# Routing at the seam between attention and experts: order of the last tiles, and constant products on TensorE

## The chip, the cores and the metric

The kernel runs on one core of a Trainium2 chip. The metric is device time in microseconds of one execution; the figure given is the median of several runs. Besides the timed runs there is one profiled execution, from which all rows here are taken.

## The reference

One layer of an encoder over 1024 tokens of width 1024, all in float32. Two attention mixers and an output projection come first; then a mixture of experts, whose routing is the subject here.

```python
h = h + jnp.concatenate([oa, ob], axis=-1) @ w_out[l]
h = h + _hierarchical_moe(_rms_norm(h, norm2_g[l]), ...)
return _rms_norm(h, final_norm_g)

def _hierarchical_moe(x, ...):            # n = 1024 tokens, 4 groups of 8 experts, TOP_K = 2
    g_logits = xt @ router_group_w + router_group_b
    g_prob = jax.nn.softmax(g_logits); g_top_p, g_top = lax.top_k(g_prob, 1)
    e_logits = xt @ router_expert_w + router_expert_b      # those of the chosen group are kept
    e_top_logit, e_top = lax.top_k(e_in_group, TOP_K)
    gates = g_top_p * jax.nn.softmax(e_top_logit, axis=-1)
    # every token goes to its two experts: (silu(x @ w_gate[e]) * (x @ w_up[e])) @ w_down[e],
    # times its gate, added up per token
```

## The kernel before

Tokens stand in eight tiles of 128 (`NT` = 8). After the attention mixers the kernel runs a routing stage, one loop over the tiles, and then 32 experts, one after the other, each with up to 128 of its tokens in one block (blocks beyond that are made in a loop at the end).

**Routing.** For tile j, `projected(j, b)` (L965) makes half b of the output projection, twelve fp32r matmuls of 512 columns from `half_product` (L833), and adds the residual. With the second half it computes the norm's factor (`rstd` on POOL), normalises the tile into `xn` on VectorE (L982), and has SP store it to `xn_d` in HBM (L983). `routed(j)` (L987) is a generator whose `yield`s let the loop put its TensorE work in between. Its steps are: transposes of the tile's two halves (L994, two steps, evicted to `xt` by ScalarE); the router's logits as sixteen passes (L1000), then on VectorE the choice of group and of two experts (L1004 to L1031), which ends in the one-hot `ohb`; the counts `pc` of earlier tokens per expert (L1034, L1035), with the gates, and per choice a matrix `put` (token to place in its expert's list) and `what` (32 columns for the token's number, 32 for its gate); last the table's product `first_at` += `put` x `what` (L1064), two fp32 matmuls. The counts need the running sum `cum` of the tiles before. `turned` (L818) normalises and transposes tile j+1 of the second mixer.

TensorE's order is written out by hand (`manual_schedule`, L1078 to L1106); the other engines' order is made by a planner that simulates the program, and in which what stands earlier in the program goes first where both are ready. `issue_after(x)` makes what is in the block, on x's engine, come behind x. After the loop over j the order is: tile 7's second transposes and logits, tile 6's counts and table, tile 7's counts and table:

```python
            for j, n in ((NT - 1, 2), (NT - 2, 2), (NT - 1, 2)):
                for _ in range(n):
                    next(routes[j])
```

**The seam.** VectorE turns the table into row numbers and gates (L1118, L1119). POOL gathers the rows of expert 0 from `xn_d` by these numbers (L1173) into `x_g`, the storage of `o_b[0]`; then it issues three weight loads (L915) and `listed` (L1068): for each tile two indirect writes of token and gate into lists in HBM, `slot_d`, whose four tensors are used in turn, so that tile 2's writes wait for those of tile 0.

**Experts.** For expert e, TensorE transposes the gathered rows (`rows_in`, L1190); ScalarE and VectorE split rows and weights into a high and a low part (`split`, L141). Twelve units of weights (512 KB each) are used, with six matmuls of 512 columns for each: eight for gate and up (L1206), four for down (L1230), the latter put among the units of the next expert. In the gate-and-up product of expert e, after its sixth unit, the rows of expert e+1 are gathered and transposed (`KR` = 5). There is one `x_g`, so a gather waits for the transposes of the one before. Weights come by SP into 39 buffers in turn; six of them (`raw_b`) and the two splitting buffers lie where the routing stage's tiles lay, and wait until those have been read for the last time.

Of the kernel before, what the change touches and what calls it, by code (L numbers as in the profile page):

```python
# [39 lines left out]
MID = 2  # L40
# [75 lines left out]
def _all(t, n, offset=0):  # L116

    return _dram(t, offset, [[0, P], [1, n]])
# [8 lines left out]
def tile_encoder(ctx, tc, I, out):  # L127
# [3 lines left out]
    def act(o, i, f=AF.Copy, **kw):  # L131
        A.activation(o, i, f, **kw)  # L132
# [162 lines left out]
    def run(g):  # L295
        for _ in g:
            pass
# [491 lines left out]
    wr = outb.tile([P, 8, 36], F32, name="wr")  # L789
    nc.sync.dma_start(wr[:, :, 0:4], I["router_group_w"][0].rearrange("(k p) n -> p k n", p=P))  # L790
    nc.sync.dma_start(wr[:, :, 4:36], I["router_expert_w"][0].rearrange("(k p) n -> p k n", p=P))
# [3 lines left out]
    G.tensor_tensor(wr, wr, gk[:, :, None].to_broadcast([P, 8, 36]), op=OP.mult)  # L795
    br = outb.tile([P, 36], F32, name="br")
    nc.sync.dma_start(br[:, 0:4], _all(I["router_group_b"], 4))
    nc.sync.dma_start(br[:, 4:36], _all(I["router_expert_b"], 32))
# [153 lines left out]
    with tc.tile_pool(name="rt", bufs=1, side="right") as rt, \  # L952
# [7 lines left out]

        def mixed(j):

            tiles[j] = turned(o_b[j // 2][:, j % 2], 1, "a")

        def projected(j, b):  # L965
# [12 lines left out]
            V.tensor_tensor(ss[:, 6:7], ss[:, 4:5], ss[:, 5:6], op=OP.add)  # L978
            rstd(ss[:, 7:8], ss[:, 6:7], D)
            for b in range(2):  # L980
                bs = slice(512 * b, 512 * b + 512)
                V.scalar_tensor_tensor(xn[:, bs], h[b], ss[:, 7:8], g2[:, bs], op0=OP.mult, op1=OP.mult)  # L982
            stores.append(nc.sync.dma_start(xn_d[P * j:P * j + P], xn).ins)  # L983
            for b in range(2):
                nc.sync.dma_start(y_d[P * j:P * j + P, 512 * b:512 * b + 512], h[b])

        def routed(j):  # L987
# [10 lines left out]
            ps = bank("c", [P, 36])  # L998
# [11 lines left out]
            e4 = wo2.tile([P, 8], F32, name="e4")  # L1010

            V.tensor_scalar(r[:, 0:1], top[:, 0:1], -1.0, None, op0=OP.mult)
            act(e4[:, 0:4], lg[:, 0:4], AF.Exp, bias=r[:, 0:1], accum_out=r[:, 1:2])
# [22 lines left out]
            V.tensor_tensor(cum, cum, ob, op=OP.add)  # L1036
            V.reciprocal(r[:, 2:3], r[:, 1:2])
            V.tensor_tensor(r[:, 7:8], top2[:, 1:2], top2[:, 0:1], op=OP.subtract)
            act(r[:, 6:7], r[:, 7:8], AF.Exp)
            V.tensor_scalar(r[:, 7:8], r[:, 6:7], 1.0, None, op0=OP.add)  # L1040
            V.reciprocal(r[:, 7:8], r[:, 7:8])
            V.tensor_tensor(r[:, 8:9], r[:, 7:8], r[:, 2:3], op=OP.mult)
            V.tensor_tensor(r[:, 9:10], r[:, 8:9], r[:, 6:7], op=OP.mult)
            V.tensor_scalar(r[:, 10:11], small[:, 35:36], -1.0, float(S - P * j), op0=OP.mult, op1=OP.add)
            puts = []
            for k in range(2):
# [4 lines left out]
                put = wo2.tile([P, P], F32, name="put")  # L1051
                (V if j >= JV else G).tensor_scalar(put, slots, r[:, 12 + k:13 + k], None, op0=OP.is_equal)
                what = wo2.tile([P, 2, NE], F32, name="what")
                for n, col in enumerate((10, 8 + k)):
                    (V if j >= JV else G).tensor_scalar(what[:, n], oh[:, k], r[:, col:col + 1], None, op0=OP.mult)
                puts.append((put, what))
# [5 lines left out]
            yield  # L1062
            for k, (put, what) in enumerate(puts):
                T.matmul(first_at, put, what.rearrange("p a b -> p (a b)"), start=(j == 0 and k == 0),  # L1064
                         stop=(j == NT - 1 and k == 1), skip_group_check=True)
# [12 lines left out]
        with tc.manual_schedule(engines={mybir.EngineType.PE}):  # L1078
            tiles[0] = first_mixed
            for j in range(NT):  # L1080
                routes.append(routed(j))
                projected(j, 0)
                if j:
                    next(routes[j - 1])
                    next(routes[j - 1])
                if (MID == 0 or j == 0) and j + 1 < NT:
                    mixed(j + 1)
                if MID != 2 and j > 1:
                    next(routes[j - 2])
                projected(j, 1)  # L1090
                if MID == 2 and j > 1:
                    next(routes[j - 2])
                if j + 1 < NT:
                    if MID and j:
                        mixed(j + 1)
                else:
                    next(routes[j])
                if j:
                    next(routes[j - 1])
                if j > 1:  # L1100
                    next(routes[j - 2])
                if j and j % 2 == 0:
                    load_until(RC + 3 * j // 2 - 1)
            for j, n in ((NT - 1, 2), (NT - 2, 2), (NT - 1, 2)):
# [11 lines left out]
        rows = lst.tile([P, NE], I32, name="rows")  # L1116
        gate = lst.tile([P, NE], F32, name="gate")
        V.tensor_scalar(rows, first_at[:, 0:NE], -1.0, float(S), op0=OP.mult, op1=OP.add)  # L1118
        V.tensor_copy(gate, first_at[:, NE:2 * NE])  # L1119
# [50 lines left out]

    def load_rows(rows):

        gathers.append(G.indirect_dma_start(out=x_g, out_offset=None, in_=xn_d[:, :],  # L1173
                                            in_offset=bass.IndirectOffsetOnAxis(ap=rows, axis=0),
                                            bounds_check=S - 1, oob_is_err=False).ins)
        return x_g
# [83 lines left out]
    with tc.manual_schedule(engines={mybir.EngineType.PE}):  # L1260
        py, gathers = [], []
        before, xg = iter(()), load_rows(rows[:, 0:1])
# [4 lines left out]
        st = rows_in(xg)  # L1267
# [109 lines left out]
```

## Time and profile before

| what | us |
|---|---|
| median of three runs | 1386.3 (1386.0 to 1390.7) |
| profiled execution | 1382.0 |
| its span, first to last instruction | 1380.4 |
| TensorE busy in the span | 1287.7 (93%) |
| VectorE busy | 1160.4 (84%) |
| ScalarE busy | 941.9 (68%) |
| GpSimd (POOL) busy | 570.5 (41%) |

The page's slices show TensorE at nine tenths in nearly every slice, and the DMA engines near full from the routing stage to the end of the experts. In the rows below, a time is that from the start of the span; x16 behind a row means that many instructions merged, whose duration runs from the first's start to the last's end; the brackets hold the idle time of the engine before it and what ended it. TensorE's matmuls overlap, so the distance of two starts, not the duration, is what one costs.

### The profile page before, as it was taken

What the parts mean: (1) busy time and instruction counts of PE and PEld (TensorE: products, weight loads), DVE (VectorE), ACT (ScalarE), POOL (GpSimd) and SP (SyncE); (2) the same over time, 40 slices, a digit from 0 to 9 for tenths busy, and PEclk for the clock granted to TensorE, in tenths of its full rate; (3) what the DMA queues carried; (4) which work ended last, traced back from release to release, by engine and by line L of the source; (5) the groups of instructions that cost most, each with busy time, mean ns of one, the idle gap of its engine ahead of it and who ended that gap; (6) DMA issues with size and microseconds to landing.
All of it is one profiled execution on the core that took longest, in us unless ns stands there. A gap on an engine that the chain in (4) does not pass through costs nothing. (4 is left out here: it accounts for less than half of the span.)

```text
span 1380.4 us, 22002 instructions
## 1 busy us (share of the span) xinstructions
PE 1287.7 (93%) x7333; PEld 1091.4 (79%) x7333; DVE 1160.4 (84%) x2001; ACT 941.9 (68%) x1390; POOL 570.5 (41%) x557
## 2 busy tenths in 40 slices
PE   5999999999998988999897999999999999999983
PEld 5999788888976877888686788878888888888862
DVE  6788997899868777887687899989999999999976
ACT  5334566655666885776443888878888888888873
POOL 5673566746566563546354611112111111111215
PEclk9999999999999999999997999999999999999997
DMA  7113321222242485567757999999999999999935
GB/s 260 62 39 85 77 69 57 67 59 49 51 135 61 123 182 149 119 145 234 287 189 266 339 373 364 350 344 360 345 368 342 354 353 358 354 347 351 361 92 224
DMA packets 213685, 301.73 MB, mean 219 GB/s; under 512 B 94436, under 2 KB 116068, under 8 KB 213569
## 3 DMA queue, kind: packets, MB, share of 16 engines
q1 hardware_dynamic: 201168, 275.01, 59.5%
q0 software_dynamic: 11968, 24.55, 6.7%
q8 instruction: 58, 0.95, 0.3%
q10 hardware_dynamic: 432, 0.75, 0.3%
q14 instruction: 59, 0.48, 0.1%
HBM read 267.85 MB, written 44.58 MB: 226 GB/s over the span
## 5 line engine op out<-in xcount | busy, mean ns | idle before, releaser
L1173 POOL DMA_INDIRECT o_b<-xn_d,rows x32 | 51.4, 1606 | 323.8 <-PE ps_a L1190 321.1
L141 DVE TENSOR_TENSOR wl<-unit,wh 128x1024 fp32r<-128x1024 f32 x130 | 156.3, 1221 | 19.9 <-ACT wh L132 19.1
L264 PE MATMUL ps_i<-wih,ul 128*128 128x256 f32 x576 | 164.5, 286 | 1.4 <-DVE ul L141 1.4
L262 PE MATMUL ps_i<-wih,uh 128*128 128x256 f32 x576 | 164.1, 285 | 0.9 <-ACT uh L132 0.8
L263 PE MATMUL ps_i<-wil,uh 128*128 128x256 f32 x576 | 163.4, 284 | 0.0
L542 POOL TENSOR_TENSOR psum<-psum,p 128x512 f32<-128x512 f32 x93 | 136.1, 1463 | 63.2 <-ACT p L132 54.8
L132 ACT ACTIVATE wh<-unit 128x1024 fp32r<-128x1024 f32 x130 | 136.6, 1062 | 34.7 <-PE ps_b L1206 12.5
L132 ACT ACTIVATE ph<-p 128x512 fp32r<-128x512 f32 x192 | 118.6, 633 | 12.0 <-DVE pl L458 5.7
L458 DVE TENSOR_TENSOR pl<-p,ph 128x512 fp32r<-128x512 f32 x93 | 98.3, 1057 | 23.9 <-ACT ph L132 23.7
L132 ACT ACTIVATE p<-ps_b 128x512 f32<-128x512 f32 x128 | 74.9, 596 | 62.1 <-PE ps_b L532 39.1
L262 PEld LDWEIGHTS ps_i<-wih,uh 128*128 128x128 f32 x576 | 111.0, 193 | 7.3 <-ACT uh L132 1.7
L263 PEld LDWEIGHTS ps_i<-wil,uh 128*128 128x128 f32 x576 | 110.9, 193 | 5.7
L264 PEld LDWEIGHTS ps_i<-wih,ul 128*128 128x128 f32 x576 | 111.0, 193 | 5.3 <-DVE ul L141 1.9
L705 POOL TENSOR_TENSOR pl<-p,ph 128x512 fp32r<-128x512 f32 x64 | 86.5, 1365 | 64.3 <-ACT ph L132 57.1
L141 DVE TENSOR_TENSOR wl<-rawc,wh 128x1024 fp32r<-128x1024 f32 x80 | 96.3, 1221 | 11.0 <-ACT wh L132 10.0
L132 ACT ACTIVATE wh<-rawc 128x1024 fp32r<-128x1024 f32 x80 | 84.4, 1062 | 20.8 <-PE ps_b L1206 8.7
L1243 POOL DMA_INDIRECT y_d<-y,rows x31 | 49.9, 1611 | 115.6 <-ACT y L132 112.3
L513 DVE TENSOR_REDUCE m<-ps_x 128x1 f32<-128x512 f32 x128 | 84.8, 678 | 7.9 <-PE ps_x L512 7.6
L1206 PE MATMUL ps_b<-wh,x_hi 128*128 128x512 f32 x256 | 86.5, 419 | 0.0
L1230 PE MATMUL ps_d<-wh,h_hi 128*128 128x512 f32 x256 | 81.0, 397 | 1.7 <-ACT h_hi L132 1.7
L1230 PE MATMUL ps_d<-wh,h_lo 128*128 128x512 f32 x256 | 81.1, 398 | 1.5 <-DVE h_lo L141 1.5
L1206 PE MATMUL ps_b<-wl,x_hi 128*128 128x512 f32 x256 | 81.3, 399 | 0.0
(323 smaller groups left out, 3864.1 us busy)
## 6 DMA issues: line engine op xcount, KB each, us to landing
unit<-in_w_up SPq DMA_DIRECT2D x47, 512.0 KB, 11.8
unit<-in_w_gate SPq DMA_DIRECT2D x42, 512.0 KB, 12.2
unit<-in_w_down SPq DMA_DIRECT2D x41, 512.0 KB, 12.1
rawc<-in_w_gate SPq DMA_DIRECT2D x30, 512.0 KB, 12.1
rawc<-in_w_down SPq DMA_DIRECT2D x26, 512.0 KB, 12.1
rawc<-in_w_up SPq DMA_DIRECT2D x24, 512.0 KB, 11.7
h_b<-in_w_down SPq DMA_DIRECT2D x19, 512.0 KB, 12.8
raw<-in_w_in SPq DMA_DIRECT2D x36, 256.0 KB, 2.9
```

The costliest lines, as they stand in the source:

```text
L132: A.activation(o, i, f, **kw)
L141: (eng or V).tensor_tensor(lo, src, hi, op=OP.subtract)
L262: T.matmul(ps[:, jj], u_hi[j][:, k], wh, start=(k == 0 and jj == 0), stop=False, skip_group_check=True)
L263: T.matmul(ps[:, jj], u_hi[j][:, k], wl, start=False, stop=False, skip_group_check=True)
L264: T.matmul(ps[:, jj], u_lo[j][:, k], wh, start=False, stop=(k == 7), skip_group_check=True)
L458: engine("pl").tensor_tensor(pl, p, ph, op=OP.subtract)
L513: V.tensor_reduce(m2[:, j, b:b + 1], ps, axis=AX.X, op=OP.max)
L542: engine("s").tensor_tensor(st["s"], st["s"], p, op=OP.add)
L705: G.tensor_tensor(pl, p, ph, op=OP.subtract)
L1173: gathers.append(G.indirect_dma_start(out=x_g, out_offset=None, in_=xn_d[:, :], in_offset=bass.IndirectOffsetOnAxis(ap=rows, axis=0), boun ...
L1206: T.matmul(st["gu"[n % 2]], lhs[:, k % 4], rhs[:, 512 * a:512 * a + 512], start=(k == 0 and i == 0), stop=(k == 7 and i == 2))
L1230: T.matmul(py[b], lhs[:, k], w[n][:, 512 * b:512 * b + 512], start=(k == 0 and i == 0), stop=(k == 3 and i == 2))
```

## The change

- The router's logits get four columns of zero weights and a bias of -1e30 between the 4 group and 32 expert columns, so one VectorE instruction makes all 40 (two and a memset before).
- The logits of tile 6 are issued within tile 7's last half product, after six of its twelve matmuls; the counts of tile 6 then stand before the table of tile 5 and before the second half of tile 7's transposes. For other tiles the order on TensorE is as before.
- For tile 7 the table's product is split: first the 32 columns of token numbers, from which the row numbers are made and the gather of expert 0 is issued; group probability, gates, the entries of the lists and the 32 gate columns follow.
- TensorE multiplies the identity by itself (128x128, fp32r), 22 times before tile 7's counts and 44 times after the gate columns, into a PSUM tile that nobody reads.
- `x_g` is zeroed after tile 3 in the program; `put` has four buffers.

```diff
-            run(half_product(1, o, ps, b))
+            for k, _ in enumerate(half_product(1, o, ps, b)):
+                if k == 1 and between:
+                    next(between)
...
-            ps = bank("c", [P, 36])
+            ps = bank("c", [P, 40])
...
-            V.memset(lg[:, 4:8], NEG)
-            for a, b in ((0, 4), (4, 36)):
-                V.scalar_tensor_tensor(lg[:, 2 * a:b + a], ps[:, a:b], ss[:, 7:8], br[:, a:b], op0=OP.mult, op1=OP.add)
+            V.scalar_tensor_tensor(lg, ps, ss[:, 7:8], br, op0=OP.mult, op1=OP.add)
...
+            for k, (_, what) in enumerate(puts):
+                E.tensor_scalar(what[:, 0], oh[:, k], r[:, 10:11], None, op0=OP.mult)
+            if not last:
+                gates()
+            for k, (put, _) in enumerate(puts):
                 tmp = wo2.tile([P, NE], F32, name="tmp")
                 V.scalar_tensor_tensor(tmp, pc, 1.0, oh[:, k], op0=OP.mult, op1=OP.mult,
                                        accum_out=r[:, 12 + k:13 + k])
+                E.tensor_scalar(put, slots, r[:, 12 + k:13 + k], None, op0=OP.is_equal)
+            V.tensor_tensor(cum, cum, ob, op=OP.add)
+            yield
+            for k, (put, what) in enumerate(puts):
+                T.matmul(first_at[:, 0:NE] if last else first_at, put,
+                         what[:, 0] if last else what.rearrange("p a b -> p (a b)"), start=(j == 0 and k == 0),
+                         stop=False, skip_group_check=True)
+            yield
+            if last:
+                group()
+                gates()
...
+            if last:
+                for k, (put, what) in enumerate(puts):
+                    T.matmul(first_at[:, NE:2 * NE], put, what[:, 1], start=False, stop=(k == 1), skip_group_check=True)
             yield
...
-                projected(j, 1)
-                if MID == 2 and j > 1:
+                if j == 0:
+                    mixed(1)
+                projected(j, 1, routes[j - 1] if j == NT - 1 else None)
+                if j > 1:
                     next(routes[j - 2])
                 if j + 1 < NT:
-                    if MID and j:
+                    if j:
                         mixed(j + 1)
+                        next(routes[j - 1])
                 else:
                     next(routes[j])
-                if j:
                     next(routes[j - 1])
                 if j > 1:
-                    next(routes[j - 2])
+                    run(routes[j - 2])
...
+            def busy(n):
+
                 for _ in range(n):
-                    next(routes[j])
-
-        x_g = o_b[0].rearrange("p a f -> p (a f)")
-        G.memset(x_g, 0.0)
+                    T.matmul(idle[:, 0:P], eyer, eyer, start=True, stop=True)
+
+            end = routes[NT - 1]
+            next(end)
+            next(end)
+            run(routes[NT - 2])
+            busy(WARM[0])
+            next(end)
+            next(end)
+            rows = lst.tile([P, NE], I32, name="rows")
+            gate = lst.tile([P, NE], F32, name="gate")
+            V.tensor_scalar(rows, first_at[:, 0:NE], -1.0, float(S), op0=OP.mult, op1=OP.add)
+            gathers = []
+            load_rows(rows[:, 0:1])
+            with tc.issue_after(gathers[0]):
+                run(end)
+            busy(WARM[1])
+            V.tensor_copy(gate, first_at[:, NE:2 * NE])
```

## Rows read from the trace of the kernel before

**Rows 1.** Stretches: us of span, busy time per engine (instructions), TensorE clock, DMA share, GB/s.

```profile
742.00:744.00 2.00, 0.75 (x7) 0.66 (x7) 1.90 (x18) 0.33 (x2) 0.00 (x0) 0.93 1.00 332
...
760.00:762.00 2.00, 2.00 (x8) 1.60 (x7) 0.86 (x1) 0.96 (x1) 0.56 (x1) 0.80 1.13 374
...
780.00:800.00 20.00, 20.00 (x94) 16.22 (x93) 18.46 (x18) 16.83 (x20) 6.05 (x4) 1.00 1.02 369
```

**Rows 2.** TensorE in order of time at the seam: start, duration, line, operands, count, idle time.

```profile
737.96 1.87 PE L1000 MATMUL ps_d<-wr,xt 128*128 128x36 f32 x16
739.67 0.64 PE L1064 MATMUL ps_i<-what,put 128*128 128x64 f32 x4
...
740.58 2.17 PE L1000 MATMUL ps_d<-wr,xt 128*128 128x36 f32 x16
...
747.44 0.19 PE L1034 MATMUL ps_i<-ohb,trib 128*128 128x32 bf16 x1
...
754.64 1.94 PE L1190 MATMUL ps_a<-mats,o_b 128*128 128x128 f32 x8 [4.95 <-DMA o_b<-xn_d,rows]
...
761.31 0.64 PE L1206 MATMUL ps_b<-wh,x_hi 128*128 128x512 f32 x2
...
766.93 1.03 PE L1190 MATMUL ps_a<-mats,o_b 128*128 128x128 f32 x8
767.73 0.71 PE L1206 MATMUL ps_b<-wh,x_hi 128*128 128x512 f32 x2
```

**Rows 3.** VectorE in order of time, 730 to 750 us.

```profile
730.62 0.38 DVE L1004 SCALAR_TENSOR_TENSOR lg<-ps_d,ss,br 128x4 f32<-128x4 f32 x2 [0.30 <-PE ps_d L1000]
...
731.50 0.75 DVE L982 SCALAR_TENSOR_TENSOR xn<-q_a,ss,g 128x512 f32<-128x512 f32 x1
732.17 0.75 DVE L982 SCALAR_TENSOR_TENSOR xn<-h_b,ss,g 128x512 f32<-128x512 f32 x1
...
733.94 0.69 DVE L974 TENSOR_TENSOR q_a<-ps_x,q_a 128x512 f32<-128x512 f32 x1 [0.23 <-PE ps_x L837]
...
735.46 0.21 DVE L1031 TENSOR_TENSOR ohb<-oh 128x32 bf16<-128x32 f32 x1
...
737.62 0.69 DVE L974 TENSOR_TENSOR h_b<-ps_x,h_b 128x512 f32<-128x512 f32 x1 [0.63 <-PE ps_x L837]
...
742.79 0.22 DVE L1004 SCALAR_TENSOR_TENSOR lg<-ps_d,ss,br 128x4 f32<-128x4 f32 x1
...
749.73 0.19 DVE L1118 TENSOR_SCALAR rows<-ps_i 128x32 int32<-128x32 f32 x1 [0.71 <-PE ps_i L1064]
```

**Rows 4.** POOL in order of time, behind the seam.

```profile
750.20 1.18 POOL L1173 DMA_INDIRECT o_b<-xn_d,rows  x1 [1.91 <-DVE gate L1119]
...
753.58 1.78 POOL L1072 DMA_INDIRECT slot_d<-ents  x1 [0.30 <-issue]
...
759.51 1.05 POOL L1173 DMA_INDIRECT o_b<-xn_d,rows  x1 [0.30 <-PE ps_b L1206]
762.53 1.70 POOL L1072 DMA_INDIRECT slot_d<-ents  x1 [1.97 <-DMA slot_d<-ents]
```

**Rows 5.** SP's DMA issues in order of time, before the seam.

```profile
737.61 0.38 SPq L915 DMA_DIRECT2D rawb<-in_w_up  x1
...
742.20 0.34 SPq L983 DMA_DIRECT2D xn_d<-xn  x1
```

**Rows 6.** DMA issues at 732.9, 742.2, 750.2, 759.5 us: size, us from issue to landing.

```profile
xn_d<-xn SPq DMA_DIRECT2D x1, 512.0 KB, 3.6
...
xn_d<-xn SPq DMA_DIRECT2D x1, 512.0 KB, 6.5
...
o_b<-xn_d,rows POOLq DMA_INDIRECT x1, 4.3
...
o_b<-xn_d,rows POOLq DMA_INDIRECT x1, 6.9
```

**Rows 7.** TensorE in order of time at 86.9 us: eight transposes, fp32r, 128x128.

```profile
86.93 0.80 PE L312 MATMUL ps_x<-eyer,q_st 128*128 128x128 f32 x8
```

More of the change, by code (lines that the diff above doesn't have):

```diff
@@ L39 @@
 WH, WL, RB = 3, 3, 6
-MID = 2
+WARM = (22, 44)
 RATE_O = 1.0
@@ L959, in tile_encoder, with load_rows, projected @@
         tiles, news, stores, routes = {}, {}, [], []
+        def load_rows(rows):
+            gathers.append(G.indirect_dma_start(out=x_g, out_offset=None, in_=xn_d[:, :],
+                                                in_offset=bass.IndirectOffsetOnAxis(ap=rows, axis=0),
+                                                bounds_check=S - 1, oob_is_err=False).ins)
+            return x_g
         def mixed(j):
             tiles[j] = turned(o_b[j // 2][:, j % 2], 1, "a")
-        def projected(j, b):
+        def projected(j, b, between=None):
             o = tiles[j]
@@ L1010, in routed, with group @@
             e4 = wo2.tile([P, 8], F32, name="e4")
-            V.tensor_scalar(r[:, 0:1], top[:, 0:1], -1.0, None, op0=OP.mult)
-            act(e4[:, 0:4], lg[:, 0:4], AF.Exp, bias=r[:, 0:1], accum_out=r[:, 1:2])
+            last = j == NT - 1
+            def group():
+                V.tensor_scalar(r[:, 0:1], top[:, 0:1], -1.0, None, op0=OP.mult)
+                act(e4[:, 0:4], lg[:, 0:4], AF.Exp, bias=r[:, 0:1], accum_out=r[:, 1:2])
+            if not last:
+                group()
             V.tensor_copy(r[:, 3:4], at[:, 0:1])
@@ L1035, in routed, with gates @@
             T.matmul(pc, oneb, cum, start=False, stop=True)
[L1036 to L1043, printed above, removed]
-            V.tensor_scalar(r[:, 10:11], small[:, 35:36], -1.0, float(S - P * j), op0=OP.mult, op1=OP.add)
-            puts = []
-            for k in range(2):
+            V.tensor_scalar(r[:, 10:11], small[:, 35:36], -1.0, float(S - P * j), op0=OP.mult, op1=OP.add)
+            puts = [(wo2.tile([P, P], F32, name="put", bufs=4), wo2.tile([P, 2, NE], F32, name="what"))
+                    for k in range(2)]
+            E = V if j >= JV else G
+            def gates():
+                V.reciprocal(r[:, 2:3], r[:, 1:2])
+                V.tensor_tensor(r[:, 7:8], top2[:, 1:2], top2[:, 0:1], op=OP.subtract)
+                act(r[:, 6:7], r[:, 7:8], AF.Exp)
+                V.tensor_scalar(r[:, 7:8], r[:, 6:7], 1.0, None, op0=OP.add)
+                V.reciprocal(r[:, 7:8], r[:, 7:8])
+                V.tensor_tensor(r[:, 8:9], r[:, 7:8], r[:, 2:3], op=OP.mult)
+                V.tensor_tensor(r[:, 9:10], r[:, 8:9], r[:, 6:7], op=OP.mult)
+                for k, (_, what) in enumerate(puts):
+                    E.tensor_scalar(what[:, 1], oh[:, k], r[:, 8 + k:9 + k], None, op0=OP.mult)
+            for k, (_, what) in enumerate(puts):
+                E.tensor_scalar(what[:, 0], oh[:, k], r[:, 10:11], None, op0=OP.mult)
+            if not last:
+                gates()
+            for k, (put, _) in enumerate(puts):
                 tmp = wo2.tile([P, NE], F32, name="tmp")
@@ L1049, in routed @@
                                        accum_out=r[:, 12 + k:13 + k])
[L1051 to L1056, printed above, removed]
+                E.tensor_scalar(put, slots, r[:, 12 + k:13 + k], None, op0=OP.is_equal)
[7 more added lines that the diff above has]
+            if last:
+                group()
+                gates()
             ent, idx = ents[:, 4 * j:4 * j + 4].rearrange("p (k f) -> p k f", k=2), ents[:, 32 + 2 * j:34 + 2 * j]
@@ L1115, in tile_encoder @@
                 load_until(NU)
[L1116 to L1119, printed above, removed]
         cum4 = lst.tile([P, 4, NE], BF, name="cum4")
@@ L1169, in merged @@
         return rows, gate
[L1171 to L1176, printed above, removed]
     def parts(raw):
@@ L1260, in tile_encoder @@
     with tc.manual_schedule(engines={mybir.EngineType.PE}):
-        py, gathers = [], []
-        before, xg = iter(()), load_rows(rows[:, 0:1])
+        py = []
+        before = iter(())
         with tc.issue_after(gathers[0]):
```

27 lines of the change are left out of this document (12 added, 15 removed).

## Prediction

> **What bounds the kernel now.** I read the slices of the page first, then the stretches of the seam, then each engine's instructions in order of time there, then the landings of single transfers. Before the seam TensorE works without a gap, and behind it too: in 780 to 800 us it is busy all 20.00 us, and the DMA engines with it [rows 1]. So the end is set by TensorE, and a microsecond won at the seam is won at the end only if nothing behind the seam takes it back. The seam is what lies between the last logits product, which starts at 740.58, and the first transposes of expert 0 at 754.64 [rows 2]. TensorE there waits for VectorE's choices of tiles 6 and 7, then for the gather of expert 0's rows. [...] One more row matters, and it is easily overlooked: expert 1's rows are gathered by POOL at 759.51 and take 6.9 us to land [rows 4, 6], which is 766.4; TensorE wants them at 766.93 [rows 2]. Only 0.5 us is spare there.
>
> **Logits of tile 6 inside the last product.** Their sixteen passes take 1.7 us (737.96 to 739.67) [rows 2]. They now start after six of the product's twelve matmuls, near 735.9 instead of 737.96, so the choice for tile 6 begins 2.0 us earlier. The price: the last product ends 1.7 us later, at about 739.3 instead of 737.6, and with it everything made from it. VectorE's addition follows it at once (737.62) and the store of the normalised tile is issued 4.6 us later (742.20) [rows 3, 5]; I put the store at 743.9, or up to 744.9 if VectorE takes tile 6's choice first. This store is what the gather reads. It took 6.5 us to land, behind weight loads that SP had issued from 737.61 on; the store of the tile before took 3.6 [rows 5, 6]. Those loads wait for the last product too and move with it, so I take 6.5: landed at 750.4, with ends 747.5 and 751.4.
>
> **TensorE's new order.** The counts of tile 6 now stand before the second half of tile 7's transposes. They need tile 6's choice, a chain of some 2.7 us on VectorE: tile 5 took from 730.62 to 735.67, with 1.4 us of normalising and 0.9 us of wait and addition in between [rows 3]. So TensorE stands still from about 739.8 to 740.5 or 741.1, and queued behind it are tile 5's entry in the table, the transposes and logits of tile 7. These logits end at 743.7 to 744.7, where they ended at 742.75 [rows 2]. Given back: tile 7's choice has VectorE nearly to itself. Before, it took from 742.79 to the counts at 747.44, 4.65 us, since tile 6's stood between [rows 2, 3]; at 2.7 us the counts of tile 7 come at 746.5 to 747.4. From them to the row numbers it was 2.29 us and to the gather 2.76 [rows 2 to 4]; with the gates, the second half of the table and the copy of the gates behind the gather, I take 1.8 to 2.3. The row numbers would allow the gather at 748.5 to 749.5, against 750.20. But the store has landed only at 750.4. This wait takes the place of the one removed, and **the gather goes out at 750.4**, with ends 748.8 and 751.5.
>
> **The constant products.** None of this form is in the trace. The nearest are eight transposes of the same shape and type, 0.80 us together, 0.08 each once the last one's 0.25 is taken off [rows 7]; doubled at half clock. So 22 cost 1.7 or 3.5 us, 44 cost 3.5 or 7.0. The 22 stand before tile 7's counts: at full clock they end by 746.5 and are hidden by the choice; at half clock they reach 748.2 and delay the counts by about 1 us, which the landing of the store would hide again. The 44 stand behind the gates' product, near 751.6, and end at 755.1 at full clock, when the rows arrive (750.4 + 4.3 = 754.7 [rows 6]). What they are worth if the clock is held: from 754.64, expert 0 reached its third unit at 761.31 [rows 2]. At full clock the transposes take 0.80 (766.93 to 767.73) and a matmul 0.234 (24 from 761.31 to 766.93) [rows 2]; with the splitting of the rows, about 1 us, and twelve matmuls, 2.8, that is 4.3 instead of 6.7 us: **2.4 us gained**.
>
> **Where this goes.** TensorE would ask for expert 1's rows 12.29 - 2.4 = 9.9 us after expert 0's transposes, which is 750.4 + 4.4 + 9.9 = 764.7. On POOL nothing of the queue between gather 0 and gather 1 is removed: three weight loads, four list writes, 9.31 us back to back [rows 4]; the two copies of tile 7's entries come in between (0.2 us each at most, otherwise idle). The later list writes can't come earlier than gather 1, since they wait for the first ones to land (762.53 [rows 4]). So rows of expert 1 land at 750.4 + 9.31 + 6.9 = 766.6, and TensorE waits 1.9 us there. It passes at 766.6, where it passed at 766.93: **-0.3 us**. Later gathers have some ten microseconds to spare, so the shift stays. Weight loads: 36 of 39 buffers are filled in this stretch, two to three experts ahead, no bound.
>
> [...] The trace has 4.3 us for the gather with the DMA engines idle and 6.9 beside weight loads [rows 6]; I go by the latter, since faster experts bring their loads forward, if anything.
>
> **The rest** costs nothing: four more logit columns (TensorE's spacing is 0.106 us at 36 columns, 1.70 over 16 [rows 2]; at most 0.2 us a tile by proportion, and none in the row, which is not set by columns alone); one VectorE instruction and a memset less per tile, where VectorE is not the bound; the zeroing of the gather's tile, moved, on POOL's idle time. A planner orders the other engines by its own simulation, so their order may shift anywhere; that is in the range, not in the sum.
>
> **The rivals.** *The clock's gain is kept* (chance 0.27): expert 1's rows come before TensorE asks, because the gather lands in 4 to 5 us or is placed sooner on POOL. Then -2.1 us at a gather at 750.4, and -3.5 if the store lands at 747.5 and the rows decide: 1382.8 to 1384.2. For it: the store of the tile before landed in 3.6. Against: POOL's queue, back to back. *The constants outlast the gather* (0.15): the hole before tile 6's counts and the one before the gates lower the clock, the 44 run at half rate, from 751.6 to 758.6, past the rows. TensorE is then late by itself: expert 1 is asked for at 758.6 + 9.9 = 768.5, +1.6 us, and +2.9 with a late gather: 1387.9 to 1389.2. It decides from the point where expert 0's transposes start after 757.0 (766.9 - 9.9). For it: the clock fell in the same place before. Against: a clock that rose after 6 us of work (754.64 to 761) would rise within the 44. *The change doesn't hold the clock* (0.10): expert 0 at half rate and no delay, 750.4 + 4.4 + 12.3 = 767.1, +0.2 us: 1386.5.
>
> **How the numbers follow.** The profiled execution took 1382.0 us, 1380.4 of it span; the runs' median is 1386.3, 4.3 us more, with 1386.0 to 1390.7 shown. I add differences to the median. Forecast, chance 0.42: 1386.3 - 0.3 = 1386.0, by its own bounds (gather 748.8 to 751.5) 1384.4 to 1387.1. The remaining 0.06 is for a shift of order elsewhere, of either sign. The range takes in the rivals on both sides and something for the scatter of the runs: 1381.5 to 1389.5. Within 0.5% (6.9 us, about what a measurement of this kernel tells from no change) lies every case worked out: the idle time of the whole seam, 11.9 us, would have to go by more than half. I leave 0.04 on either side.
>
> **What would show it.** Right: the last product ending near 739.3; the gather issued when the store lands, not when the row numbers are there; full clock in expert 0; a wait of 1 to 2 us for expert 1's rows, absent before. Wrong: gather 0 well before 750; gather 1 less than 15 us behind it in landing; constants still running when expert 0's rows are there; or TensorE's pace behind the seam other than before.

## The result, and the profile after

The changed kernel takes 1394.3 us, median of 13 runs (1389.9 to 1400.0), against 1386.0 (1382.8 to 1390.7) for the kernel before, timed alongside: a ratio of 1.0068, interval 1.0053 to 1.0083. It is slower by 8.3 us. The forecast was 1386.0 with a range up to 1389.5, so the time lies outside, on the side to which 0.04 had been given.

The profiled execution took 1390.5 us, with a span of 1388.7. Stretches of it, the same three as in [rows 1] and two more (us of span, busy time per engine, TensorE clock, DMA share, GB/s):

```profile
742.00:744.00 2.00, 2.00 (x12) 2.00 (x11) 1.39 (x7) 0.00 (x0) 0.00 (x0) 0.54 1.05 381
...
760.00:762.00 2.00, 2.00 (x10) 1.87 (x9) 0.00 (x0) 0.00 (x0) 1.08 (x2) 0.50 1.02 389
...
764.00:766.00 2.00, 2.00 (x6) 1.57 (x6) 1.29 (x2) 0.60 (x1) 1.64 (x2) 0.50 0.14 43
766.00:768.00 2.00, 2.00 (x10) 1.63 (x9) 0.85 (x1) 1.53 (x2) 1.39 (x3) 0.98 0.03 5
...
780.00:800.00 20.00, 19.66 (x93) 15.73 (x92) 18.36 (x19) 17.10 (x22) 6.66 (x5) 1.00 0.96 333
```

The stretch at 742 is already at half clock (0.54, where it was 0.93), with TensorE fully busy; so is all that lies between (0.50 in each 2 us from 744 to 766), and the clock is back only at 766 (0.98; each count of busy time is the profile's, which models the ends of matmuls). TensorE in order of time at the seam, as in [rows 2] (start, duration, line, operands, count, idle time before and what ended it):

```profile
734.40 1.87 PE L1012 MATMUL ps_d<-wr,xt 128*128 128x40 f32 x16
...
737.66 0.63 PE L1006 MATMUL ps_b<-mats,q_a 128*128 128x128 f32 x4
740.21 0.18 PE L1050 MATMUL ps_i<-ohb,trib 128*128 128x32 bf16 x1 [1.92 <-DVE ohb L1047]
...
741.18 2.68 PE L1012 MATMUL ps_d<-wr,xt 128*128 128x40 f32 x16
...
744.51 4.93 PE L1141 MATMUL ps_x<-eyer 128*128 128x128 f32 x22
749.25 0.25 PE L1050 MATMUL ps_i<-ohb,trib 128*128 128x32 bf16 x1
...
752.43 9.63 PE L1141 MATMUL ps_x<-eyer 128*128 128x128 f32 x44
762.12 1.97 PE L1228 MATMUL ps_a<-mats,o_b 128*128 128x128 f32 x8
...
774.17 1.07 PE L1228 MATMUL ps_a<-mats,o_b 128*128 128x128 f32 x8 [0.59 <-PE ps_c L1244]
```

Two things are to be seen. The 44 constants (L1141) run from 752.43 to 762.12 at half clock, and expert 0's transposes follow without idle time: TensorE isn't waiting for rows there, the rows are waiting for TensorE. And each constant costs 9.69 / 44 = 0.22 us. Then VectorE's row numbers, SP's store of the normalised tile, and POOL's gathers (L966) and list writes (L1102), which answer [rows 3 to 5]:

```profile
751.31 0.19 DVE L1152 TENSOR_SCALAR rows<-ps_i 128x32 int32<-128x32 f32 x1 [0.79 <-PE ps_i L1081]
...
742.56 0.34 SPq L995 DMA_DIRECT2D xn_d<-xn  x1
...
751.79 1.18 POOL L966 DMA_INDIRECT o_b<-xn_d,rows  x1 [10.62 <-DVE rows L1152]
...
755.54 1.15 POOL L1102 DMA_INDIRECT slot_d<-ents  x1 [0.30 <-issue]
...
762.79 0.96 POOL L1102 DMA_INDIRECT slot_d<-ents  x1 [1.41 <-DMA slot_d<-ents]
...
767.84 1.45 POOL L966 DMA_INDIRECT o_b<-xn_d,rows  x1 [0.30 <-issue]
```

Between the gathers of expert 0 and 1 lie eight list writes, not four, the fifth with its wait for the first ones to land; the distance is 16.05 us where it was 9.31.

Spans begin with work that the change doesn't touch and that differs from one execution to the next, so I count from a point of the seam: the start of tile 6's first transposes (733.74 before, 732.13 after). Differences of starts in the timelines, us (in the first column the end of the logits); "gather 0" is POOL's instruction, "expert 0" and "expert 1" are their first transposes on TensorE:

| kernel | logits of tile 7 end | counts of tile 7 | gather 0 | gather 1 behind it | expert 0 | expert 1 | median, us | ratio |
|---|---|---|---|---|---|---|---|---|
| before | 9.01 | 13.70 | 16.46 | 9.31 | 20.90 | 33.19 | | |
| after | 11.73 | 17.12 | 19.66 | 16.05 | 29.99 | 42.04 | 1394.3 | 1.0068 |
| no_const | 13.35 | 16.48 | 19.04 | 9.90 | 23.75 | 36.74 | 1388.0 | 1.0018 |
| const_first | 11.65 | 17.05 | 19.59 | 9.91 | 24.18 | 37.38 | 1387.8 | 1.0025 |
| const_last | 11.55 | 14.68 | 17.77 | 16.91 | 27.58 | 41.74 | 1394.2 | 1.0070 |
| wide | 11.61 | 17.07 | 19.12 | 9.92 | 26.31 | 36.92 | 1385.3 | 1.0006 |
| counts_back | 10.74 | 14.36 | 18.01 | 9.91 | 22.28 | 35.91 | 1388.2 | 1.0018 |
| gates_last | 9.02 | 13.49 | 16.49 | 9.89 | 21.16 | 35.11 | 1384.8 | 0.9999 |
| lists_late | 13.35 | 16.49 | 19.05 | 6.82 | 23.64 | 35.38 | 1384.9 | 0.9993 |
| const_lists_late | 11.64 | 17.03 | 19.57 | 12.59 | 29.90 | 41.30 | 1390.6 | 1.0033 |
| before_lists_late | 9.01 | 13.70 | 16.46 | 6.97 | 21.21 | 32.12 | 1382.7 | 0.9976 |
| gl_lists_late | 9.02 | 13.49 | 16.04 | 6.82 | 20.63 | 31.57 | 1382.3 | 0.9979 |
| gl_wide | 9.03 | 13.49 | 16.37 | 9.91 | 21.69 | 34.93 | 1388.5 | 1.0013 |
| wide_best | 9.03 | 13.49 | 16.21 | 6.58 | 21.41 | 31.54 | 1380.9 | 0.9969 |

Ratios are to the kernel before, timed alongside each time; each place at the seam is read from one profiled execution. Between expert 1's transposes and the end of the span lie 613.5 us before and 614.5 after. So the loss stands at the seam: 42.04 - 33.19 = 8.9 us in the profiled executions, 8.3 in the medians. Of it 3.2 us is a later gather 0 (19.66 - 16.46), 5.9 the time from gather 0 to expert 0's transposes (10.33 against 4.44), and -0.2 expert 0 itself (12.05 against 12.29).

### The profile page after: what moved, and what is told of

The parts are those of the page before. It is cut to its first block, busy times and chain, and to the rows that moved or that the text cites. A ratio compares the mean times of both kernels' runs of the same rounds, so it can differ in the third digit from the quotient of the medians.

```text
span 1388.7 us, 22127 instructions
## 1 busy us (share of the span) xinstructions
PE 1300.1 (94%) x7403; PEld 1104.4 (80%) x7403; DVE 1159.6 (84%) x1985; ACT 942.5 (68%) x1390; POOL 567.2 (41%) x559
## 5 line engine op out<-in xcount | busy, mean ns | idle before, releaser
L966 POOL DMA_INDIRECT o_b<-xn_d,rows x32 | 52.5, 1641 | 338.4 <-PE ps_a L1228 327.0
L458 DVE TENSOR_TENSOR pl<-p,ph 128x512 fp32r<-128x512 f32 x93 | 94.8, 1021 | 26.2 <-ACT ph L132 26.1
L1244 PE MATMUL ps_b<-wh,x_hi 128*128 128x512 f32 x256 | 86.9, 421 | 0.0
```

Source lines behind the costliest of these rows:

```text
L458: engine("pl").tensor_tensor(pl, p, ph, op=OP.subtract)
L1244: T.matmul(st["gu"[n % 2]], lhs[:, k % 4], rhs[:, 512 * a:512 * a + 512], start=(k == 0 and i == 0), stop=(k == 7 and i == 2))
```

## The experiments

**Without constants, and with either half of them.** `WARM` holds the two counts.

```diff
-WARM = (22, 44)
+WARM = (0, 0)      # no_const
+WARM = (22, 0)     # const_first
+WARM = (0, 44)     # const_last
```

> The changed kernel without its 66 constant products, everything else as changed. Theory A (the constants ran at half clock, did not raise it, and stood in line: 4.7 us before tile 7's counts, 9.6 us before expert 0, and they pushed the gather of expert 1 behind four more list writes): the counts of tile 7 come 2.3 us earlier, the gather of expert 0 near 749.5 us, expert 0 starts near 754 at half clock, the gather of expert 1 is 9.7 us behind that of expert 0 and lands near 766; time 1384.5 to 1386.5, ratio to the kernel before 0.999 to 1.0005. Rival B (the loss comes from the new order of the last tiles and the late gates, not from the constants): 1391 or more, ratio 1.003 or more.

> Only the 22 constants before tile 7's counts, none behind. A: at half clock they end 2.3 us after the choice of tile 7, so the gather of expert 0 goes out near 751.8, expert 0 starts near 756.1 at half clock, expert 1's rows are transposed near 768.4: 1387 to 1388.5, 1.5 to 2.5 us over the run without constants. B: as without constants.

> Only the 44 constants behind the gates' product. A: at half clock they take 9.6 us from about 750.1, expert 0 starts near 759.8 instead of 754, and the gather of expert 1, behind eight list writes, lands near 772: 1390 to 1392.5, 5 to 7 us over the run without constants. Had they held or raised the clock: 1385 to 1388. B: as without constants.

Measured: 1.0018 (1.0000 to 1.0036) without, 1.0025 (1.001 to 1.004) with the first 22, 1.0070 (1.0048 to 1.0093) with the last 44. So the 44 carry most of the loss, 6.2 us by the medians of const_last and no_const; the rest, about 2.5 us, is there without any constant, which is between theory A (at most 1.0005) and rival B (at least 1.003). The 22 alone add nothing that can be told from no_const. TensorE of const_last, and two stretches of four us (TensorE's busy time, its clock, DMA share, GB/s):

```profile
749.59 9.63 PE L1141 MATMUL ps_x<-eyer 128*128 128x128 f32 x44
759.28 1.97 PE L1228 MATMUL ps_a<-mats,o_b 128*128 128x128 f32 x8
...
773.44 1.94 PE L1228 MATMUL ps_a<-mats,o_b 128*128 128x128 f32 x8 [3.07 <-DMA o_b<-xn_d,rows]
```

```profile
768.00:772.00 4.00, 2.38 (x11) 1.00 0.88 266
772.00:776.00 4.00, 2.56 (x10) 0.58 1.04 389
```

Here the clock came back within expert 0 (0.70 in 760 to 764, 1.00 in 764 to 768), but TensorE then stood 3.1 us for expert 1's rows and did their transposes at half clock (1.94 us; 0.58 in 772 to 776): the gain is taken back, and more. Between its two gathers lie eight list writes, as in the changed kernel, so this run doesn't separate the length of the constants from the order on POOL; const_lists_late, below, does. The 22 delay the counts of tile 7 by 17.12 - 14.68 = 2.4 us, yet gather 0 in const_last goes only 1.9 us earlier than in the changed kernel, since a DMA holds it there (below, at gates_last).

**Wide constants.** Half as many products, each over four copies of the identity (512 columns instead of 128), in the same places.

```diff
-WARM = (22, 44)
+WARM = (11, 22)
...
-                    T.matmul(idle[:, 0:P], eyer, eyer, start=True, stop=True)
+                    T.matmul(idle.rearrange("p (a b) -> p a b", a=4), eyer,
+                             eyer[:, None, :].to_broadcast([P, 4, P]), start=True, stop=True)
```

> The constants with 512 columns (the identity four times side by side, read with stride 0), 11 and 22 of them, which at half clock is the same time as 22 and 44 of 128 columns. A1 (the width of the product decides whether this work raises the clock): the clock is full again before expert 0, the 22 take near 5 us instead of 9.6, and expert 1's rows, landing 9.7 + 6.9 us behind the first gather, set the pace: 1385.5 to 1388.5. A2 (such work does not raise the clock whatever its width): half clock until expert 0, 1389 to 1393, as with 128 columns.

Measured: 1.0006 (0.9994 to 1.0018), 1385.3 us, 9 us below the changed kernel and just under the range of A1. TensorE, and stretches of it:

```profile
744.51 4.97 PE L1141 MATMUL ps_x<-eyer 128*128 128x512 f32 x11
...
751.61 6.89 PE L1141 MATMUL ps_x<-eyer 128*128 128x512 f32 x22
758.56 1.09 PE L1229 MATMUL ps_a<-mats,o_b 128*128 128x128 f32 x8
...
769.17 1.06 PE L1229 MATMUL ps_a<-mats,o_b 128*128 128x128 f32 x8 [0.31 <-DMA o_b<-xn_d,rows]
```

```profile
744.00:748.00 4.00, 4.00 (x12) 0.50 1.02 397
748.00:752.00 4.00, 3.03 (x16) 0.84 0.16 66
752.00:756.00 4.00, 4.00 (x13) 0.59 0.52 178
756.00:760.00 4.00, 3.65 (x20) 0.99 0.84 278
```

The first eleven take as long as the 22 narrow ones (4.97 and 4.93 us), from the same start. The clock rises as they end (0.84 in 748 to 752); behind the 22 narrow ones it doesn't (0.50 in 748 to 752, in the changed kernel and in const_first). It is down again after the pauses that follow (TensorE busy 3.03 of 4 us in 748 to 752, then 0.59 in 752 to 756), and up once more as the second group ends (0.99 in 756 to 760). It too outlasts the gather: expert 0 starts 7.2 us behind gather 0, against 4.7 in no_const. But expert 0 then runs at full clock (1.00 from 760 on, its transposes in 1.09 us), and expert 1 follows 10.6 us behind, not 12.3; a wait of 0.3 us for expert 1's rows ends this gain. What is shown is that wide constants don't cost what narrow ones cost. That they gain something over no constants isn't shown at the seam: expert 1 stands at 36.92, in no_const at 36.74. The median is 2.7 us under that of no_const, but the intervals of the two ratios overlap.

**The order of the last tiles.** Both kernels have no constants. counts_back puts the counts of tile 6 behind the logits of tile 7 again, with tile 6's logits still within the last product; gates_last has TensorE's old order, and keeps row numbers and gather first, gates last.

```diff
 # counts_back, with WARM = (0, 0)
-                    next(routes[j - 1])
...
+            next(routes[NT - 2])
             run(routes[NT - 2])
 # gates_last, with WARM = (0, 0)
-                projected(j, 1, routes[j - 1] if j == NT - 1 else None)
+                projected(j, 1)
...
+            next(routes[NT - 2])
             run(routes[NT - 2])
```

> No constants, and the counts of tile 6 again behind tile 7's logits as before the change; the logits of tile 6 stay within the last product. Theory C (of the 3 us that are left without constants, most come from the counts of tile 6 standing in front of tile 7's second transposes: 1.9 us of idle TensorE, a clock that falls during them, logits of tile 7 that take 3.5 us instead of 2.2): the logits of tile 7 end near 741.5, the gather of expert 0 then waits for the store of the last tile and goes out near 749.2, expert 1's rows are transposed near 766: 1384 to 1386, 2 to 3 us under the run without constants. Rival D (the 3 us come from the gates behind the gather and from POOL's order): as without constants, 1387 to 1389.

> No constants and TensorE's order as before the change; only the one-instruction logits, and row numbers and gather ahead of gates and gate columns, are kept. C: the gather of expert 0 goes out 0.5 to 1 us earlier than in the kernel before, near 749.4, and expert 1's gather follows 9.9 us behind, so 1384 to 1385.5, ratio 0.9985 to 1.000. D: slower than the kernel before by 1 to 3 us.

Measured: counts_back 1388.2 us, 1.0018 (1.0003 to 1.0034), as no_const: theory C fell, and the time is that of rival D. gates_last 1384.8 us, 0.9999 (0.9984 to 1.0015), within C's range. The hole before tile 6's counts isn't the cost of the order, then: without it the store of the tile is still issued at 10.33 us (8.46 before, 8.39 in gates_last) and gather 0 at 18.01. The two kernels differ in one thing, where tile 6's logits stand, and with them within the last product the median is 3.4 us higher (2.6 by the ratios). So that is what costs, and not D's gates behind the gather, which gates_last has too. And rows-first by itself gains nothing (gather 0 at 16.49, before at 16.46), because the gather waits for something else. VectorE's row numbers, SP's store and POOL's gather in gates_last:

```profile
744.40 0.19 DVE L1153 TENSOR_SCALAR rows<-ps_i 128x32 int32<-128x32 f32 x1 [0.50 <-PE ps_i L1081]
...
737.24 0.34 SPq L995 DMA_DIRECT2D xn_d<-xn  x1
...
739.03 0.34 SPq L918 DMA_DIRECT2D h_b<-in_w_down  x1
...
745.34 1.18 POOL L966 DMA_INDIRECT o_b<-xn_d,rows  x1 [4.18 <-DMA h_b<-in_w_down]
```

The row numbers are there at 744.59, and the gather goes out at 745.34, 8.1 us behind the store's issue, held by a DMA. The profile names the weight load issued right behind the store, not the store; the two aren't told apart here. With row numbers as the last to come, 0.48 us lay between the two (751.31 and 751.79 in the changed kernel), so this wait costs about half a us here. In counts_back, with the later store, 1.56 us lie between them (750.74 and 752.30), so it costs 1.1. In the profiled execution of gates_last expert 1 comes 1.9 us later than before, behind a wait of 1.6 for its rows; the median doesn't show that loss.

**List writes behind later gathers.** In four kernels (no_const, the changed kernel, the kernel before, gates_last) the list writes are given out two tiles at a time, behind the gathers of experts 1 to 4, instead of all of them behind gather 0.

```diff
-            for e in range(NT):
-                listed(e)
...
+                    if e < 4:
+                        with tc.issue_after(gathers[-1]):
+                            for j in (2 * e, 2 * e + 1):
+                                listed(j)
```

> The changed kernel without constants, the list writes moved behind the gathers of experts 1 to 4, so that expert 1's gather follows three weight loads only. If that gather, behind four list writes, is what expert 1 waits for (1.1 us in the trace without constants): it goes out 4.9 us behind the first one, the wait is gone, 1.1 us under the run without constants. If something else sets the start of expert 1: no change.

> The changed kernel with its 66 constants, the list writes moved behind the gathers of experts 1 to 4. Theory E (the constants set the start of expert 0, and the gather of expert 1 behind eight list writes costs only the 0.6 us that TensorE waits for it in the trace): 0.5 to 1 us under the changed kernel, ratio to the kernel before 1.0055 to 1.007. Rival F (POOL's queue, eight list writes instead of four before expert 1's gather, is a large part of the loss): 3 us or more under the changed kernel, ratio 1.0045 or less.

> The kernel before with nothing changed but the list writes, moved behind the gathers of experts 1 to 4. By the trace of before, TensorE had 0.5 us to spare at expert 1's rows: no change, ratio 0.9995 to 1.0005. If the landing of that gather varies from run to run so that it is often late: up to 1.5 us faster, ratio 0.999.

> TensorE's order as before, gates last, no constants, and the list writes late. In the run with gates last alone TensorE waited 1.6 us for expert 1's rows; with the gather of expert 1 right behind the weight loads that wait is gone and only the half-rate start of expert 0 remains: ratio 0.998 to 0.9995. If gates last brings nothing even then: 1.000.

Measured: no_const falls by 3.2 us to 0.9993 (0.9979 to 1.0008), gates_last by 2.6 to 0.9979 (0.9963 to 0.9994), the changed kernel by 3.7 to 1.0033 (1.0018 to 1.0049), and the kernel before gets to 0.9976 (0.9960 to 0.9991) by this alone. In each, gather 1 goes out 2.3 to 3.5 us earlier behind gather 0, and in none of the four does TensorE wait for expert 1's rows. The gain is larger than was expected for no_const (1.1 us) and for the kernel before, where it lies outside both forecasts (0.9995 and 0.999 at the lowest). For the changed kernel theory E, that the constants alone set its time, would have left 1.0055 to 1.007; the measured 1.0033 speaks for its rival. How the gain arises is shown only in part: in the profiled executions expert 1 comes 1.36 us earlier than in no_const, 0.7 earlier than in the changed kernel (41.30 against 42.04) and 1.07 earlier than in the kernel before, where the medians fall by 3.2, 3.7 and 3.4 (for gates_last 3.54 and 2.6). The kernel before doesn't wait for expert 1's rows in its profile; whether it does in its slower executions wasn't seen.

const_lists_late and lists_late differ in the 66 constants alone, and in neither does TensorE wait for a gather at expert 1. So they give the price of the constants by themselves: 5.9 us at expert 1 (41.30 against 35.38), 5.7 in the medians.

**Together.** wide_best is gates_last with wide constants in TensorE's four holes of the seam and the late list writes, that is gl_lists_late with constants; gl_wide is the same with the lists in their place.

```diff
-WARM = (22, 44)
+WARM = (6, 2, 3, 11)
...
+            busy(WARM[0])
+            next(routes[NT - 2])
+            busy(WARM[1])
             run(routes[NT - 2])
-            busy(WARM[0])
             next(end)
+            busy(WARM[2])
             next(end)
...
-            busy(WARM[1])
+            busy(WARM[3])
```

> TensorE's order as before the change, gates last, list writes late, and constants of 512 columns: 6 before and 2 behind tile 6's counts, 3 between tile 7's counts and its row columns, 11 behind the gate columns, all meant to fit into idle time. If the clock can be held by such work and expert 1's gather no longer waits: expert 0 starts near 753.8 at full clock, expert 1's rows are transposed near 763.8, 3 us earlier than before: 1381 to 1383. If the constants delay the choice or the clock falls all the same: 1385 to 1388.

> The fastest version (order as before, gates last, list writes late, 512-column constants) with the list writes back in their place. By the prediction's argument, that the clock's gain is given back at expert 1's gather: the gather follows 9.9 us behind the first and lands 6.5 to 7 us later, so expert 1 starts about 1.5 us later than with the lists late; ratio 0.998 to 0.9995, against 0.997. If the gain does not depend on the gather: 0.997.

Measured: wide_best 1380.9 us, 0.9969 (0.9955 to 0.9984), the fastest of all; gl_wide 1388.5, 1.0013 (0.9994 to 1.0031), with runs from 1381.4 to 1390.8, above both of its forecasts. TensorE of gl_lists_late (expert 0's transposes and its third unit of weights) and of wide_best, then POOL of wide_best:

```profile
753.91 1.94 PE L1229 MATMUL ps_a<-mats,o_b 128*128 128x128 f32 x8 [3.76 <-DMA o_b<-xn_d,rows]
...
759.23 0.63 PE L1245 MATMUL ps_b<-wh,x_hi 128*128 128x512 f32 x2
```

```profile
748.45 4.49 PE L1141 MATMUL ps_x<-eyer 128*128 128x512 f32 x11
753.00 1.09 PE L1232 MATMUL ps_a<-mats,o_b 128*128 128x128 f32 x8
...
757.51 0.63 PE L1248 MATMUL ps_b<-wh,x_hi 128*128 128x512 f32 x2
...
763.13 1.03 PE L1232 MATMUL ps_a<-mats,o_b 128*128 128x128 f32 x8
```

```profile
747.80 1.18 POOL L966 DMA_INDIRECT o_b<-xn_d,rows  x1 [3.85 <-DVE rows L1156]
...
754.38 1.08 POOL L966 DMA_INDIRECT o_b<-xn_d,rows  x1 [3.13 <-PE ps_a L1232]
755.77 1.04 POOL L1102 DMA_INDIRECT slot_d<-ents  x1 [0.30 <-issue]
```

The constants end when the rows come, expert 0 takes 10.13 us, and gather 1 now waits only for the buffer, that is for expert 0's transposes. The clock isn't held through the seam (0.67 in 744 to 748, 0.50 in 748 to 752), but it is back as expert 0 starts (0.98 in 752 to 756). Against gl_lists_late, which has no constants, expert 0 takes 0.8 us less (10.13 against 10.94) and starts 0.8 later (21.41 against 20.63): expert 1 stands at 31.54 and 31.57. The intervals of the two ratios (0.9969 and 0.9979) overlap. So what the constants add to late list writes isn't shown; most of the 0.3% is there without them. In gl_wide the same clock is won and lost again:

```profile
755.81 1.06 PE L1232 MATMUL ps_a<-mats,o_b 128*128 128x128 f32 x8 [0.34 <-DMA o_b<-xn_d,rows]
...
769.05 1.94 PE L1232 MATMUL ps_a<-mats,o_b 128*128 128x128 f32 x8 [2.97 <-DMA o_b<-xn_d,rows]
```

```profile
764.00:768.00 4.00, 2.08 (x9) 1.00 0.88 295
768.00:772.00 4.00, 2.95 (x11) 0.52 1.06 397
772.00:776.00 4.00, 4.00 (x13) 0.62 0.69 251
```

TensorE asks for expert 1's rows 10.3 us after expert 0's transposes, waits 2.97 us, and goes on at half clock. The pair differs in the list writes alone: 7.6 us by the medians, 6.1 by the ratios. The profiles show 3.4 of it at expert 1 (1.5 had been expected) and 5.6 at expert 2, whose transposes stand at 54.5 against 48.9: the stretch at half clock adds 2.2.

**Three more profiled executions of the changed kernel**, as its median lies 3.8 us above its profiled execution (that of the kernel before lies 4.0 above).

> The changed kernel once more, for its spread. Theory G: the median of 1394 against the 1390.5 of its profiled execution comes of longer waits for the gather of expert 1 in other executions; a wait of 2 to 4 us at expert 1's rows, a stretch at half clock right behind it, and 1393 to 1399 us. Rival H: the first transposes of expert 1 stand some 42 us behind those of tile 6 as in the first profile, and the time differs elsewhere.

> The same test a second time. Theory G: the longer the wait for expert 1's rows (0.6 us in the first profile), the longer the execution. Rival H: the wait and the time do not go together over these executions.

> The same test a third time. Theory G: the longer the wait for expert 1's rows (0.6 us in the first profile), the longer the execution. Rival H: the wait and the time do not go together over these executions.

Measured: 1389.9, 1394.3 and 1389.8 us; the kernel before, once beside them, 1386.9. Theory G fell: in none of them does the profile list idle time of TensorE before expert 1's transposes, not in the longest either. TensorE and POOL of the longest:

```profile
764.98 1.97 PE L1228 MATMUL ps_a<-mats,o_b 128*128 128x128 f32 x8
...
776.65 1.03 PE L1228 MATMUL ps_a<-mats,o_b 128*128 128x128 f32 x8
```

```profile
754.65 1.18 POOL L966 DMA_INDIRECT o_b<-xn_d,rows  x1 [10.22 <-DVE rows L1152]
...
770.51 1.63 POOL L966 DMA_INDIRECT o_b<-xn_d,rows  x1 [0.30 <-issue]
```

The seam is the same in all four executions: expert 1 stands 41.3, 41.3 and 41.6 us behind tile 6's transposes (42.0 in the first), 8.1 to 8.9 later than in the one profile of the kernel before, close to the difference of the medians, 8.3. The longer execution was late before the seam already (tile 6's transposes at 735.38, not at 731.7 to 732.1). What made the other timed runs reach 1400 isn't settled; the lowest runs of the two kernels differ by 7.1 us, the profiled ones by 8.4.

## Why the prediction was wrong, point by point

- **Where the end is set: right.** What TensorE loses at the seam it loses at the end: 8.9 us at expert 1, 8.4 in the profiled times, 8.3 in the medians. (One side reading was wrong: the idle time of the seam in the kernel before is 9.1 us, 2.05 + 1.22 + 0.90 + 4.95; the 11.9 that were given hold TensorE's work in it too.)
- **Logits within the last product: the store right, its price put at almost nothing.** The store was put 1.7 to 2.7 us later; it is 10.43 - 8.46 = 2.0 later. But this was taken as covered, with gather 0 only 0.2 us later than before. In counts_back, where the store's delay stands by itself, gather 0 goes out 1.55 us later (18.01 against 16.46), held by a DMA until 7.7 us behind the store's issue, where 6.5 were taken. counts_back against gates_last gives 2.6 to 3.4 us of time with what follows from it; the intervals of the two ratios overlap, so the size is uncertain. This is the second, smaller part of the loss.
- **The hole before tile 6's counts: mis-sized.** 0.7 to 1.3 us were worked out, 1.92 was measured, and tile 7's logits end 2.7 us later, not 1.0 to 2.0. VectorE's addition for the last half (0.68 us at 737.81) still stands within tile 6's choice. The chain for tile 7 took 3.1 us in no_const (13.35 to 16.48) where 2.7 was taken, and 2.56 us from the counts to the gather where 1.8 to 2.3 were.
- **The gather goes out when the store has landed: failed in the changed kernel.** Row numbers at 751.31 released it, 3.2 us later than before on the seam's scale, and not the store. The wait itself exists and is worth half a us in gates_last and const_last, 1.1 in counts_back.
- **The price of a constant: mis-sized, by the row it was taken from.** Eight transposes of the same shape had 0.80 us together, 0.08 each with the last one's 0.25 taken off (the median of single ones at L312 is 0.248), 0.16 doubled [rows 7]; measured were 4.74 / 22 = 0.215 and 9.69 / 44 = 0.220 at a clock of 0.50. A nearer row, at half clock, stood in the rows all the same: expert 0's eight transposes, 1.94 us at 754.64 [rows 2], where the clock was 0.50 (754 to 756), which is 0.21 each with the same 0.25 taken off. It gives 9.3 us for the 44, and by the rival's own sum expert 1 at 751.6 + 9.3 + 9.9 = 770.8, 3.9 us late where 1.6 were worked out.
- **"A clock that rose after 6 us of work (754.64 to 761) would rise within the 44": this is the step that failed.** 4.9 and 9.7 us of back-to-back narrow products left the clock at 0.50, with TensorE busy 2.00 of every 2 us. It rose at 766, after 512-column matmuls had begun at 763.97. In wide, the same time in 512-column products, from the same start, had it up as they ended (0.84 in 748 to 752, where the changed kernel has 0.50). So with the 44 in place TensorE was late by itself: the rival *the constants outlast the gather* is what happened. It had been priced with 7.0 us of constants ending at 758.6 and 1.6 to 2.9 us of loss; 9.7 us after a later gather ended at 762.1 (763.7 on the scale of the kernel before), and expert 0 stood 5.9 us further behind its gather. The 66 constants by themselves cost 5.5 to 5.7 us of the 8.3 (const_lists_late against lists_late, by ratios and by medians).
- **What a kept clock is worth: near for that one execution, too high as a price.** 2.4 us were worked out for expert 0, from 0.80, about 1 and 2.8, which add up to 4.6 and not to 4.3, so 2.1. wide_best has its third unit at 4.51 and 12.29 - 10.13 = 2.2 less than the kernel before. But in the profile of the kernel before the clock rises late (0.50 in each 2 us from 744 to 760, 1.00 in 762 to 764), and expert 0 reaches its third unit after 6.67 us; in gl_lists_late, with no constants and half clock at the start as well (transposes of 1.94 us), after 5.32. Against that run a full clock from the start saves 0.8 us.
- **POOL between the gathers: failed as a fact of the order, right as a mechanism.** That "nothing of the queue between gather 0 and gather 1 is removed" was taken to mean that nothing is added; the planner put four more list writes before gather 1 in the changed kernel and in const_last. "The later list writes can't come earlier than gather 1" had gather 1 in its old place; here it came behind them, at 767.84, while the fifth went out at 762.79. Where the order stayed (gl_wide) TensorE waited as argued, 2.97 us against the 1.9 worked out. Not foreseen: in gl_wide and const_last the clock is down as that wait ends (0.52 in 768 to 772 and 0.58 in 772 to 776, transposes of 1.94 us), so it costs more than its length. The first rival, *the clock's gain is kept*, needs the gather sooner on POOL. wide_best has that, at 1380.9 us, below the rival's 1382.8 to 1384.2; but its gain against the kernel before is mostly that of the list writes (gl_lists_late, 1382.3).
- **Landing of the gather: near, on the short side.** The prediction took 6.9 us beside weight loads, and not the 4.3 of gather 0 [rows 6], which went out with the DMA engines idle (share 0.00 in 750 to 752). In wide, const_last and gl_wide, where TensorE waits for it, it is 7.1 to 8.7 us from issue to first transpose (761.29 to 769.17, 766.38 to 773.44, 760.40 to 769.05).

## What to carry over

Work put into a hole to hold a clock has a price at the low clock too (0.22 us a product here, where a row at full clock had given 0.08); take that price from a row at that clock, and cut the filler so that it ends before what it waits for even if the clock never rises. Before giving a queue a new order, list what stands between two transfers that the bottleneck needs: moving list writes that nobody waits for behind the gathers gave 0.24% alone, and with them in the old place the constants of wide_best ended in a wait of 2.97 us. Compare a kernel with filler to the same kernel without it, not only to the one before both changes: the fastest version here owes most of its gain to the list writes. A time won behind one wait is only won if the next transfer can come sooner as well.

## What the runs showed of the hardware

In 9.7 us of 128-column fp32r products, back to back, the granted clock stayed at 0.50 in the changed kernel (752 to 762) and in const_last (748 to 760); in const_lists_late the 44 took the same 9.63 us. In wide the 512-column ones, in the same places, ended in stretches with 0.84 (748 to 752) and 0.99 (756 to 760). Why, the runs don't tell: the two differ in width, and also in number, 22 products against 11 in the first place, over 4.9 and 5.0 us, and each of the changed kernel's 66 has a load of the identity of its own, of 0.333 us. And the clock isn't the same behind the same wait. Expert 10 begins with a wait of 2.72 us for VectorE in both kernels; before (first line of each pair the end of the wait, second the first matmuls behind it) and after:

```profile
919.57 0.16 PE L1144 MATMUL ps_a<-fullb,trib 128*128 128x2 bf16 x1 [2.72 <-DVE mrow L1152]
...
919.67 0.71 PE L1206 MATMUL ps_b<-wh,x_hi 128*128 128x512 f32 x2
```

```profile
926.74 0.16 PE L1189 MATMUL ps_a<-fullb,trib 128*128 128x2 bf16 x1 [2.72 <-DVE mrow L1197]
...
926.84 1.20 PE L1244 MATMUL ps_b<-wh,x_hi 128*128 128x512 f32 x2
```

After the same wait the pair of matmuls takes 0.71 us in one (clock 1.00 from 916 to 924) and 1.20 in the other (0.81 in 924 to 928, 0.76 in 928 to 932), and expert 10 loses 1.4 us to the kernel before's profile there. One profiled execution can thus be off by more than a us through a place that no edit touches; the differences above are read at the seam for that reason, and their totals from medians.
